# Two low parts per narrow-expert chunk move from VectorE to GpSimd, and TensorE takes them half a piece later

## The chip, the cores and the metric

The kernel runs on one core of a Trainium2 chip. Its engines each run their own queue of instructions: TensorE (PE, whose weight loads the profile calls PEld), VectorE (DVE), ScalarE (ACT), GpSimd (POOL) and SyncE (SP), which here issues the weight loads from memory. The metric is the device time of one execution in microseconds (us).

## What is computed

A decoder trunk of two layers over 256 tokens of width 1024: attention, a dense SwiGLU, an mLSTM mixer, and then the part that this change touches, a top-2-of-8 expert SwiGLU with a hidden width of 3584:

```python
def swiglu(h, wg, wu, wd):
    return (jax.nn.silu(h @ wg) * (h @ wu)) @ wd

def moe_swiglu(h, router, wg, wu, wd):
    ...
    for e in range(N_EXPERTS):
        y = y + combine[..., e:e + 1] * swiglu(h, wg[e], wu[e], wd[e]).astype(jnp.float32)
    return y.astype(h.dtype)
```

Everything is float32. The weights of all eight experts are read, 44 MB for each expert.

## The kernel before, in words

**Two parts for each number.** TensorE multiplies in the format fp32r, and the kernel keeps the accuracy by splitting each number into a high part (the number rounded to fp32r) and a low part (what the rounding left). For each weight, ScalarE makes the high part `whi` by a copy (line 204, in `split`), and VectorE makes the low part `wlo` by a subtraction of `whi` from the raw weight (line 208). Both inputs of that subtraction, `raw` and `whi`, lie in the on-chip memory SBUF.

**Experts, chunks, pieces, halves.** The eight experts come one after another, wide and narrow by turns (`WIDE`): a wide one has up to 128 tokens, a narrow one (1, 3, 5 and 7) up to 64. An expert has seven chunks of 512 hidden columns. A chunk loads six pieces of 1 MB: two of the gate matrix, two of the up matrix, two of the down matrix. Each piece is split and multiplied in two halves of 128x1024 numbers, so a chunk has twelve half pieces: gate 0 to 3, up 4 to 7, and then the four of the down product of the chunk before. In a narrow expert the stationary operand `xg` holds the high and the low part of 64 tokens side by side, so that a half piece takes four matmuls of 512 columns: two with `whi` (line 228) and then two with `wlo` (line 230), in `mm2s`. A wide expert takes six (lines 220, 221 and 223, in `mm3s`).

**The order.** `Stream.run` walks a list of half pieces, in an order that is kept on every engine. Before half piece n is multiplied, `fill` has issued the split of half piece n+3, so ScalarE and VectorE work up to three half pieces ahead. There are four buffers for `whi` and four for `wlo` (`NB_HI`, `NB_LO`), and ten for the raw pieces (`NB_RAW`): SyncE loads the next piece when both halves of an old one have been split. `Stream.soon(n, f)` puts a step off: it counts down at the end of each half piece, the present one too. Through it come, once for each narrow chunk, the turning of the two products onto the other axis (eight matmuls, line 1313), their product (VectorE, line 1320) and its low part (line 1325); in chunk 3 also the gathering of the next expert's tokens (line 1517), and after an expert's last chunk the scattering of its result (line 1445).

In `mm2s`, the matmuls of a narrow half piece:

```python
for o, l, r, start, _ in terms:
    nc.tensor.matmul(o, l, r[0], start=start, stop=False)
for o, l, r, _, stop in terms:
    nc.tensor.matmul(o, l, r[1], start=False, stop=stop)
```

GpSimd has no work in the experts' stretch but a small transfer and two products at the very end. Earlier, in the attention, it makes six low parts of weights (line 208 too) and one at line 599.

Of the kernel before, what the change touches and what calls it, by code (L numbers as in the profile page):

```python
# [23 lines left out]
KB = D // P  # L24
# [22 lines left out]
WIDE = (True, False, True, False, True, False, True, False)  # L47
# [22 lines left out]
def trunk(ctx: ExitStack, tc: tile.TileContext, out, rope_inv, x, positions, norm_mix, norm_ffn,  # L70
# [3 lines left out]
    nc = tc.nc  # L74
# [35 lines left out]
    def ps(tag, shape, dtype=F32):  # L110
        return psum.tile(shape, dtype, name=uniq("ps_" + tag), tag=tag, bufs=4)


    def load(src, shape, key=None):
        if key in early:
            return early.pop(key)
        n = int(np.prod(shape[1:]))
        t = weights.tile([P, 2048], F32, name=uniq("raw"), tag="raw", bufs=NB_RAW)
        v = t[:, :n]
        if len(shape) == 3:  # L120
            v = v.rearrange("p (k c) -> p k c", k=shape[1])
        nc.sync.dma_start(v, src)
        return v
# [18 lines left out]
    class Stream:  # L142
# [2 lines left out]
        def __init__(self):  # L145
            self.items, self.ready, self.later, self.at = [], [], [], 0

        def piece(self, src, shape, use, after=None, key=None):

            raw = []  # L150

            def get(j, sub):
                if not raw:
                    raw.append(load(None if key in early else src(), shape, key))
                v = raw[0]
                if isinstance(v, list):
                    return [w.rearrange("p a c -> p (a c)") for w in split(v[2 * j:2 * j + 2], sub)]
                return split(v[:, 2 * j:2 * j + 2] if shape[1] == 4 else v[:, j], sub)

            self.items.append((partial(get, 0), lambda w: use(0, w), None))  # L160
            self.items.append((partial(get, 1), lambda w: use(1, w), after))
# [25 lines left out]
    def split(v, sub=nc.vector):  # L187
        vs = v if isinstance(v, list) else [v]
        shape = [P, 2, 512] if isinstance(v, list) else list(v.shape)
        n = int(np.prod(shape[1:]))  # L190
        hi = weights.tile([P, 1024], F32R, name=uniq("whi"), tag="whi", bufs=NB_HI)[:, :n]
        lo = weights.tile([P, 1024], F32R, name=uniq("wlo"), tag="wlo", bufs=NB_LO)[:, :n]
        if len(shape) == 3:
            hi = hi.rearrange("p (k c) -> p k c", k=shape[1])
            lo = lo.rearrange("p (k c) -> p k c", k=shape[1])
        if chores and begun[0]:
            chores.pop(0)()
        with ExitStack() as order:
            if held:
                for ins in held.pop(0):  # L200
                    order.enter_context(tc.issue_after(ins))
            for i, part in enumerate(vs):
                h, l = (hi[:, i], lo[:, i]) if isinstance(v, list) else (hi, lo)
                nc.scalar.copy(h, part)  # L204
                if sub == PUT_OFF:
                    put_off.append(partial(nc.vector.tensor_sub, l, part, h.bitcast(F32)))
                elif sub:
                    sub.tensor_sub(l, part, h.bitcast(F32))  # L208
        return hi, lo
# [7 lines left out]
    def mm3s(terms):  # L217

        for o, l, r, start, _ in terms:
            nc.tensor.matmul(o, l[0], r[0], start=start, stop=False)  # L220
            nc.tensor.matmul(o, l[1], r[0], start=False, stop=False)  # L221
        for o, l, r, _, stop in terms:
            nc.tensor.matmul(o, l[0], r[1], start=False, stop=stop)  # L223

    def mm2s(terms):

        for o, l, r, start, _ in terms:
            nc.tensor.matmul(o, l, r[0], start=start, stop=False)  # L228
        for o, l, r, _, stop in terms:
            nc.tensor.matmul(o, l, r[1], start=False, stop=stop)  # L230


    ident = const([P, P], F32, "ident")
# [100 lines left out]
    def rsqrt_steps(ssq, scales, name):  # L334

        n = ssq.shape[1]
        v = tmp([P, n], F32, name + "_v")
        y = tmp([P, n], F32, name + "_y")
        t = tmp([P, n], F32, name + "_t")
        yi = y.bitcast(I32)  # L340
        steps = [partial(nc.vector.tensor_scalar, v[:, a:b], ssq[:, a:b], 1.0 / width, EPS, op0=OP.mult, op1=OP.add)
                 for a, b, width in scales]
        steps += [partial(nc.vector.tensor_scalar, yi, v.bitcast(I32), 1, None, op0=OP.logical_shift_right),
                  partial(nc.vector.tensor_scalar, yi, yi, -1.0, float(0x5F3759DF), op0=OP.mult, op1=OP.add)]
        each = [slice(i, i + 1) for i in range(n)]
        if n <= NT:
            steps.append(partial(nc.vector.tensor_scalar, v, v, -0.5, None, op0=OP.mult))
        for _ in range(3):
            if n <= NT:
                steps += [partial(nc.vector.scalar_tensor_tensor, t[:, c], y[:, c], v[:, c], y[:, c],  # L350
                                  op0=OP.mult, op1=OP.mult) for c in each]
                steps += [partial(nc.vector.scalar_tensor_tensor, y[:, c], t[:, c], 1.5, y[:, c],
                                  op0=OP.add, op1=OP.mult) for c in each]
            else:
                steps += [partial(nc.vector.scalar_tensor_tensor, t, y, -0.5, y, op0=OP.mult, op1=OP.mult),
                          partial(nc.vector.tensor_mul, t, t, v),
                          partial(nc.vector.scalar_tensor_tensor, y, t, 1.5, y, op0=OP.add, op1=OP.mult)]
        return y, steps

    def rsqrt_pool(ssq, width, name):  # L360

        v, y, t = (tmp(list(ssq.shape), F32, name + part) for part in ("_v", "_y", "_t"))
        yi = y.bitcast(I32)
        nc.vector.tensor_scalar(v, ssq, 1.0 / width, EPS, op0=OP.mult, op1=OP.add)
        nc.vector.tensor_scalar(yi, v.bitcast(I32), 1, None, op0=OP.logical_shift_right)
        nc.vector.tensor_scalar(yi, yi, -1.0, float(0x5F3759DF), op0=OP.mult, op1=OP.add)
        nc.gpsimd.tensor_scalar(v, v, -0.5, None, op0=OP.mult)
        for _ in range(3):
            nc.gpsimd.tensor_mul(t, y, v)
            nc.gpsimd.tensor_mul(t, t, y)  # L370
            nc.gpsimd.tensor_scalar(t, t, 1.5, None, op0=OP.add)
            nc.gpsimd.tensor_mul(y, y, t)
        return y
# [56 lines left out]
    def at(pair, *idx):  # L430
        return pair[0][idx], pair[1][idx]
# [158 lines left out]
    r, more = rsqrt_steps(ssq, [(0, NT, Q_LORA), (NT, 2 * NT, KV_LORA)], "lat")  # L590
# [25 lines left out]
    def q_rotary(wq4, b):  # L616
        p = ps("a", [P, 4, ROPE])
        for k in range(2):
            mm3(p, tok(cT, k, b), at(wq4[k], slice(None), slice(None), slice(NOPE, QK)), k == 0, k == 1)
        return p  # L620
# [7 lines left out]
    for a in range(2):  # L628
        for b in range(NT):
            nc.tensor.matmul(rows_p[:, a, b * P:(b + 1) * P], r[:, 2 * a + b:2 * a + b + 1].to_broadcast([P, P]), ident,  # L630
                             start=True, stop=True)
# [65 lines left out]
    for half in range(2):  # L697
# [6 lines left out]
        for b in range(NT):  # L704
            p = q_rotary(wq4, b) if half else qr_first[b]
# [3 lines left out]
        for h in range(hs, hs + 4, 2):  # L709
            p = ps("a", [P, 2, S])  # L710
# [6 lines left out]
        for h in range(hs, hs + 4, 2):  # L717
            p = ps("a", [P, 2, S])
# [3 lines left out]
        for b in range(NT):  # L722
            p = ps("a", [P, 4, VD])
# [52 lines left out]
    piece = []  # L776
# [60 lines left out]
    r = x_ffn.rsqrt("ffn0")  # L837
# [79 lines left out]
    for k in range(KB):  # L917
        for n in range(2):
            nc.tensor.matmul(rows_p, wg[:, k].rearrange("p a c -> p (a c)"), aT[n][:, k],
                             start=k + n == 0, stop=k == KB - 1 and n == 1)  # L920
# [35 lines left out]
    for blocks, src in ((slice(0, 2), Mr), (slice(2, 3), Mr[:, P:])):  # L956
        n = src.shape[1] // P
        src = src.rearrange("p (a c) -> p a c", a=n)
# [43 lines left out]
    for h in range(HEADS):  # L1002
        e = ps("b", [P, 3, P])
# [3 lines left out]
                         start=False, stop=True)  # L1007
# [30 lines left out]
    r = rsqrt_pool(hsq, VD, "head")  # L1038
# [211 lines left out]
    def expert_chunk(e, c):  # L1250

        for w, after in ((moe_w_gate, gated), (moe_w_up, upped)):
            p = []
            for i in range(2):
                moe.piece(lambda w=w, i=i: w[expert_at(e), c, i], [P, 4, 512], partial(inner, e, i, p),
                          partial(after, e, c, p) if i else None)

    def inner(e, i, p, j, w):
        if i + j == 0:
            p.append(ps("a", [P, 512]))  # L1260
        xg = tokens[e][0]
        k = 4 * i + 2 * j
        if not WIDE[e]:
            mm2s([(p[0], xg[:, k + kk], at(w, slice(None), kk), k + kk == 0, k + kk == KB - 1) for kk in range(2)])
            return
        mm3s([(p[0], (xg[:, 0, k + kk], xg[:, 1, k + kk]), at(w, slice(None), kk), k + kk == 0, k + kk == KB - 1)
              for kk in range(2)])
# [179 lines left out]
    moe = Stream()  # L1447
# [103 lines left out]
    xg = bigt([P, KB, P], F32, "xg")  # L1551
    with tc.If(rv > 0):
        for e in range(NE):
# [5 lines left out]
            for c in range(NCH):  # L1559
                gu = []  # L1560
                for w in (moe_w_gate[e], moe_w_up[e]):
                    p = ps("a", [P, 512])
# [14 lines left out]
                for i in range(2):  # L1577
                    raw = load(moe_w_down[e, 2 * c + i], [P, 2, D])
                    for h in range(2):
                        for kk in range(2):  # L1580
                            j = 2 * i + kk
                            nc.tensor.matmul(acc[h], hT[:, j], raw[:, kk, h * 512:(h + 1) * 512],
                                             start=c == 0 and j == 0, stop=c == NCH - 1 and j == 3)
            for h in range(2):
                ye = tmp([P, 512], F32, "ye_hi")
                nc.scalar.copy(ye, acc[h])
                for b in range(NT):
                    p = ps("a", [P, 512])
# [61 lines left out]
```

## Time and profile before

| what | value |
|---|---|
| time, median of 3 runs | 1414.47 us (1413.94 to 1414.93) |
| the profiled execution's own time | 1414.09 us |
| its span in the profile | 1412.4 us |
| experts' stretch, first to last narrow chunk | about 575 to 1395 us of the span |
| busy: PE, DVE, ACT, POOL | 97%, 88%, 71%, 4% of the span |
| TensorE's granted clock, mean over the span | 0.995 |
| read from memory | 436.67 MB, 310 GB/s over the span |

The span is the time from the first to the last instruction of the profiled execution; 1.7 us of its own time lie outside it. A busy share is the time in which an engine had an instruction in work. The matmuls overlap each other in the record, so that TensorE counts as busy when it is not at its peak. Line numbers are those of the kernel before; those of the change lie up to eight lines later.

### The profile page before, as it was taken

The page shows a single profiled execution, that of the slowest core. Times are in us where ns is not written, and L with a number is a line of the kernel's source. Part 1 is how long each engine was busy: PE and PEld are TensorE (multiplying, and loading weights), DVE is VectorE, ACT ScalarE, POOL GpSimd, SP SyncE. Part 2 cuts the span into 40 slices and gives each one's busy share as a digit, 9 for nine tenths or more (in the row PEclk, how much of TensorE's full clock was granted, in tenths as well). Part 3 has the DMA queues.
Part 4 walks back from the last instruction along what each step waited for, and adds up shares of the span by engine and source line. Part 5 has one row for each costly group of instructions (what it writes and reads, how often), then busy time and mean ns, then how long its engine had stood idle before and what let it go on. Part 6 is the DMA issues. An engine that isn't in the chain of part 4 may idle for free.

```text
span 1412.4 us, 18954 instructions
## 1 busy us (share of the span) xinstructions
PE 1363.4 (97%) x6457; PEld 1086.2 (77%) x6457; DVE 1249.6 (88%) x1604; ACT 999.1 (71%) x1272; POOL 51.4 (4%) x99
## 2 busy tenths in 40 slices
PE   7999999999999899999999999999999999999995
PEld 5788888888887688877778877778887777888673
DVE  6859998956978888999998899999889999899996
ACT  5545444445864777888877788977788897778995
POOL 4300000000020100000000000000000000000000
PEclk9999999999999999999999999999999999999998
DMA  9456666555457777999999999999999999999991
GB/s 361 160 209 208 212 211 218 194 180 197 175 197 309 275 291 266 353 368 390 421 380 338 352 368 412 399 420 365 335 366 370 400 416 399 334 371 380 381 416 36
DMA packets 63614, 439.06 MB, mean 311 GB/s; under 512 B 7489, under 2 KB 7654, under 8 KB 11798
## 3 DMA queue, kind: packets, MB, share of 16 engines
q1 hardware_dynamic: 61478, 428.15, 79.2%
q0 software_dynamic: 1872, 9.61, 1.9%
q8 instruction: 52, 0.85, 0.2%
q14 instruction: 52, 0.43, 0.1%
q10 hardware_dynamic: 160, 0.02, 0.0%
HBM read 436.67 MB, written 1.08 MB: 310 GB/s over the span
## 4 chain that ended last, share of the span: by engine, by line
PE 84%; DVE 9%; issue 2%; ACT 2%; POOL 1%; DMA 0%; DVEq 0%; ACTq 0%; POOLq 0%
PE ps_a L220 11%; PE ps_a L221 11%; PE ps_a L223 11%; PE ps_a L230 6%; PE ps_a L228 5%; PE ps_b L230 4%; DVE wlo L208 4%; PE ps_b L220 4%; PE ps_b L228 4%; PE ps_b L221 4%; PE ps_b L223 3%; PE ps_a L1313 3%; PE ps_b L213 3%; PE ps_b L215 3%; PE ps_b L214 3%
## 5 line engine op out<-in xcount | busy, mean ns | idle before, releaser
L208 DVE TENSOR_TENSOR wlo<-raw,whi 128x1024 fp32r<-128x1024 f32 (+1 forms) x783 | 919.8, 1224 | 96.5 <-ACT whi L204 91.1
L204 ACT CAST whi<-raw 128x1024 fp32r<-128x1024 f32 (+1 forms) x792 | 804.1, 1049 | 256.2 <-PE ps_a L221 112.2
L220 PE MATMUL ps_a<-whi,xg 128*128 128x512 f32 x448 | 177.0, 395 | 1.1 <-ACT whi L204 1.1
L221 PE MATMUL ps_a<-whi,xg 128*128 128x512 f32 x448 | 176.3, 393 | 0.0
L230 PE MATMUL ps_a<-wlo,xg 128*128 128x512 f32 x448 | 147.8, 411 | 8.3 <-DVE wlo L208 8.2
L223 PE MATMUL ps_a<-wlo,xg 128*128 128x512 f32 x448 | 140.2, 394 | 1.9 <-DVE wlo L208 1.9
L228 PE MATMUL ps_a<-whi,xg 128*128 128x512 f32 x448 | 140.2, 394 | 0.0
L230 PEld LDWEIGHTS ps_a<-wlo,xg 128*128 128x128 f32 x448 | 77.4, 188 | 50.8 <-DVE wlo L208 38.3
L223 PEld LDWEIGHTS ps_a<-wlo,xg 128*128 128x128 f32 x448 | 83.8, 188 | 22.7 <-DVE wlo L208 3.2
L220 PEld LDWEIGHTS ps_a<-whi,xg 128*128 128x128 f32 x448 | 84.1, 188 | 21.0 <-ACT whi L204 1.5
L221 PEld LDWEIGHTS ps_a<-whi,xg 128*128 128x128 f32 x448 | 84.1, 188 | 19.7 <-DVE xg L1517 0.5
L228 PEld LDWEIGHTS ps_a<-whi,xg 128*128 128x128 f32 x448 | 84.0, 188 | 19.2
L220 PE MATMUL ps_b<-whi,hT_hi 128*128 128x512 f32 x224 | 91.2, 407 | 0.0
L220 PE MATMUL ps_a<-whi,xT_hi 128*128 128x512 f32 x224 | 88.5, 395 | 0.1
L221 PE MATMUL ps_b<-whi,hT_lo 128*128 128x512 f32 x224 | 88.4, 394 | 0.0
L221 PE MATMUL ps_a<-whi,xT_lo 128*128 128x512 f32 x224 | 88.3, 394 | 0.0
L768 DVE CUSTOM_DVE_ANT_0 junk<-raw,wr 128x1024 bf16<-128x1024 f32 x64 | 78.1, 1221 | 2.0 <-DMA raw<-mlstm_w_out_dram 1.4
L230 PE MATMUL ps_b<-wlo,hT_hi 128*128 128x512 f32 x224 | 75.4, 416 | 0.5 <-DVE wlo L208 0.5
L228 PE MATMUL ps_b<-whi,hT_hi 128*128 128x512 f32 x224 | 73.2, 406 | 1.0 <-ACT whi L204 1.0
L223 PE MATMUL ps_b<-wlo,hT_hi 128*128 128x512 f32 x224 | 70.3, 395 | 0.0
L223 PE MATMUL ps_a<-wlo,xT_hi 128*128 128x512 f32 x224 | 69.9, 392 | 0.0
L213 PE MATMUL ps_b<-whi,hT_hi 128*128 128x512 f32 x152 | 60.9, 401 | 0.0
(443 smaller groups left out, 1882.2 us busy)
## 6 DMA issues: line engine op xcount, KB each, us to landing
raw<-moe_w_gate_dram SPq DMA_DIRECT2D x112, 1024.0 KB, 6.3
raw<-moe_w_up_dram SPq DMA_DIRECT2D x112, 1024.0 KB, 6.8
raw<-moe_w_down_dram SPq DMA_DIRECT2D x105, 1024.0 KB, 7.3
raw<-ffn_w_gate_dram SPq DMA_DIRECT2D x14, 1024.0 KB, 4.9
raw<-ffn_w_up_dram SPq DMA_DIRECT2D x14, 1024.0 KB, 5.1
raw<-ffn_w_down_dram SPq DMA_DIRECT2D x14, 1024.0 KB, 4.8
raw<-mlstm_w_in_dram SPq DMA_DIRECT2D x12, 1024.0 KB, 4.8
raw<-mla_w_out_dram SPq DMA_DIRECT2D x4, 1024.0 KB, 7.7
```

The costliest lines, as they stand in the source:

```text
L204: nc.scalar.copy(h, part)
L208: sub.tensor_sub(l, part, h.bitcast(F32))
L213: nc.tensor.matmul(o, l[0], r[0], start=start, stop=False)
L214: nc.tensor.matmul(o, l[0], r[1], start=False, stop=False)
L215: nc.tensor.matmul(o, l[1], r[0], start=False, stop=stop)
L220: nc.tensor.matmul(o, l[0], r[0], start=start, stop=False)
L221: nc.tensor.matmul(o, l[1], r[0], start=False, stop=False)
L223: nc.tensor.matmul(o, l[0], r[1], start=False, stop=stop)
L228: nc.tensor.matmul(o, l, r[0], start=start, stop=False)
L230: nc.tensor.matmul(o, l, r[1], start=False, stop=stop)
L768: nc.vector.tensor_tensor_reduce(junk, a, b, 1.0, 0.0, OP.mult, OP.add, acc)
L1313: nc.tensor.matmul(t[:, n, j], src[:, j * P:(j + 1) * P], twice, start=n + j == 0, stop=n + j == 4)
```

## The change

In a narrow expert, the low part of the second half of the first gate piece (half piece 1) and of the first up piece (half piece 5) is made on GpSimd in place of VectorE: 2 of the 12 half pieces of a chunk, 56 in all. The same subtraction of the same shape goes to another queue. For half piece 1 and 5 of a narrow chunk, the two matmuls with the low part are put off by `soon(2)`, which is to the end of the next half piece.

```diff
-        def piece(self, src, shape, use, after=None, key=None):
+        def piece(self, src, shape, use, after=None, key=None, on_pool=None):
...
             def get(j, sub):
+                if j == on_pool:
+                    sub = nc.gpsimd
...
-    def mm2s(terms):
+    def mm2s(terms, later=None):
 
         for o, l, r, start, _ in terms:
             nc.tensor.matmul(o, l, r[0], start=start, stop=False)
-        for o, l, r, _, stop in terms:
-            nc.tensor.matmul(o, l, r[1], start=False, stop=stop)
+
+        def low_parts():
+            for o, l, r, _, stop in terms:
+                nc.tensor.matmul(o, l, r[1], start=False, stop=stop)
+
+        later(low_parts) if later else low_parts()
...
-                          partial(after, e, c, p) if i else None)
+                          partial(after, e, c, p) if i else None, on_pool=None if WIDE[e] or i else 1)
...
-            mm2s([(p[0], xg[:, k + kk], at(w, slice(None), kk), k + kk == 0, k + kk == KB - 1) for kk in range(2)])
+
+            mm2s([(p[0], xg[:, k + kk], at(w, slice(None), kk), k + kk == 0, k + kk == KB - 1) for kk in range(2)],
+                 partial(moe.soon, 2) if (i, j) == (0, 1) else None)
```

On VectorE, in the gate and the first up half pieces of one chunk of expert 1, before (`raw_5559` and `raw_5588` are the two gate pieces, `raw_5609` and `raw_5629` the up pieces; a `wlo` is a low part):

```order
L208 TENSOR_TENSOR wlo_5562<-raw_5559,whi_5561 128x1024
L208 TENSOR_TENSOR wlo_5581<-raw_5559,whi_5580 128x1024
L208 TENSOR_TENSOR wlo_5591<-raw_5588,whi_5590 128x1024
L1320 TENSOR_TENSOR hT_lo_5579<-ps_a_5569,hT_lo_5579 128x256
L208 TENSOR_TENSOR wlo_5601<-raw_5588,whi_5600 128x1024
L208 TENSOR_TENSOR wlo_5612<-raw_5609,whi_5611 128x1024
L1325 TENSOR_TENSOR hT_hi_5578<-hT_lo_5579,hT_hi_5578 128x4x64
L208 TENSOR_TENSOR wlo_5622<-raw_5609,whi_5621 128x1024
L208 TENSOR_TENSOR wlo_5632<-raw_5629,whi_5631 128x1024
```

The same place on VectorE with the change:

```order
L210 TENSOR_TENSOR wlo_5562<-raw_5559,whi_5561 128x1024
L210 TENSOR_TENSOR wlo_5591<-raw_5588,whi_5590 128x1024
L1328 TENSOR_TENSOR hT_lo_5579<-ps_a_5569,hT_lo_5579 128x256
L210 TENSOR_TENSOR wlo_5601<-raw_5588,whi_5600 128x1024
L210 TENSOR_TENSOR wlo_5612<-raw_5609,whi_5611 128x1024
L1333 TENSOR_TENSOR hT_hi_5578<-hT_lo_5579,hT_hi_5578 128x4x64
L210 TENSOR_TENSOR wlo_5632<-raw_5629,whi_5631 128x1024
```

`wlo_5581` and the second half of `raw_5609` have gone from VectorE's queue. They now stand on GpSimd's, one behind the other with nothing between, for all narrow chunks of an expert.

On TensorE, the four gate half pieces of the same chunk, before:

```order
L228 MATMUL ps_a_5604<-whi_5561,xg_4725 128x512 x2
L230 MATMUL ps_a_5604<-wlo_5562,xg_4725 128x512 x2
L228 MATMUL ps_a_5604<-whi_5580,xg_4725 128x512 x2
L230 MATMUL ps_a_5604<-wlo_5581,xg_4725 128x512 x2
L228 MATMUL ps_a_5604<-whi_5590,xg_4725 128x512 x2
L230 MATMUL ps_a_5604<-wlo_5591,xg_4725 128x512 x2
L228 MATMUL ps_a_5604<-whi_5600,xg_4725 128x512 x2
L230 MATMUL ps_a_5604<-wlo_5601,xg_4725 128x512 x2
```

And with the change:

```order
L230 MATMUL ps_a_5604<-whi_5561,xg_4725 128x512 x2
L234 MATMUL ps_a_5604<-wlo_5562,xg_4725 128x512 x2
L230 MATMUL ps_a_5604<-whi_5580,xg_4725 128x512 x2
L230 MATMUL ps_a_5604<-whi_5590,xg_4725 128x512 x2
L234 MATMUL ps_a_5604<-wlo_5591,xg_4725 128x512 x2
L234 MATMUL ps_a_5604<-wlo_5581,xg_4725 128x512 x2
L230 MATMUL ps_a_5604<-whi_5600,xg_4725 128x512 x2
L234 MATMUL ps_a_5604<-wlo_5601,xg_4725 128x512 x2
```

The two matmuls with `wlo_5581` have moved behind all four of half piece 2. Their number is the same.

## Rows read from the trace of the kernel before

**Rows 1.** The page's parts 1 and 5: engines, costliest groups.

```profile
PE 1363.4 (97%) x6457; PEld 1086.2 (77%) x6457; DVE 1249.6 (88%) x1604; ACT 999.1 (71%) x1272; POOL 51.4 (4%) x99
...
L208 DVE TENSOR_TENSOR wlo<-raw,whi 128x1024 fp32r<-128x1024 f32 (+1 forms) x783 | 919.8, 1224 | 96.5 <-ACT whi L204 91.1
```

**Rows 2.** Busy time by chunk: a wide one, expert 1's, one of expert 7.

```profile
core 0: us, PE busy (x) PEld busy (x) DVE busy (x) ACT busy (x) POOL busy (x), PEclk, DMA share, GB/s
558.20:575.39 17.19, 17.19 (x77) 13.93 (x76) 15.25 (x15) 13.39 (x14) 0.00 (x0) 1.00 0.96 368
575.39:590.68 15.29, 15.29 (x69) 12.41 (x68) 13.73 (x16) 13.24 (x16) 0.00 (x0) 1.00 0.85 303
590.68:608.05 17.37, 17.05 (x81) 13.58 (x80) 16.79 (x19) 14.32 (x19) 0.00 (x0) 1.00 0.98 388
608.05:623.20 15.15, 14.21 (x67) 10.48 (x65) 15.15 (x16) 13.23 (x16) 0.00 (x0) 1.00 0.85 321
623.20:637.49 14.29, 14.01 (x66) 10.33 (x65) 14.29 (x15) 13.14 (x18) 0.00 (x0) 1.00 1.01 423
637.49:656.08 18.59, 17.71 (x104) 14.90 (x104) 16.64 (x20) 14.52 (x22) 0.00 (x0) 1.00 0.98 391
...
684.37:700.33 15.96, 15.68 (x72) 11.76 (x72) 15.96 (x17) 13.54 (x18) 0.00 (x0) 1.00 1.01 420
...
1336.90:1351.19 14.29, 14.04 (x65) 10.36 (x65) 14.29 (x15) 13.12 (x18) 0.00 (x0) 1.00 1.01 420
```

**Rows 3.** Timeline of VectorE in one chunk of expert 7: start, length, line.

```profile
1337.02 11.45 DVE L208 TENSOR_TENSOR wlo<-raw,whi 128x1024 fp32r<-128x1024 f32 x10
1348.37 0.43 DVE L1320 TENSOR_TENSOR hT_lo<-ps_a,hT_lo 128x256 f32<-128x256 f32 x1
1348.70 2.37 DVE L208 TENSOR_TENSOR wlo<-raw,whi 128x1024 fp32r<-128x1024 f32 x2
```

**Rows 4.** Timeline of TensorE in the same chunk, first waiting, then not.

```profile
1339.44 0.30 PEld L230 LDWEIGHTS ps_a<-wlo,xg 128*128 128x128 f32 x2 [0.37 <-DVE wlo L208]
...
1343.41 1.00 PE L1313 MATMUL ps_a<-twice,act 128*128 128x64 f32 x8
...
1345.11 0.71 PE L228 MATMUL ps_b<-whi,hT_hi 128*128 128x512 f32 x2
...
1348.00 0.63 PE L228 MATMUL ps_a<-whi,xg 128*128 128x512 f32 x2
1348.46 0.63 PE L230 MATMUL ps_a<-wlo,xg 128*128 128x512 f32 x2
```

**Rows 5.** Timeline of GpSimd's low parts in the attention, some merged.

```profile
18.60 2.19 POOL L208 TENSOR_TENSOR wlo<-raw,whi 128x896 fp32r<-128x896 f32 x1 [11.70 <-ACT whi L204]
...
24.32 2.35 POOL L599 TENSOR_TENSOR wlo<-raw,whi 128x1024 fp32r<-128x1024 f32 x1
...
39.02 4.19 POOL L208 TENSOR_TENSOR wlo<-raw,whi 128x768 fp32r<-128x768 f32 x2 [4.30 <-ACT whi L204]
```

**Rows 6.** Timeline of VectorE beside those of group 5.

```profile
17.72 1.09 DVE L208 TENSOR_TENSOR wlo<-raw,whi 128x896 fp32r<-128x896 f32 x1
18.73 2.08 DVE L516 SCALAR_TENSOR_TENSOR mix_y<-mix_t,mix_y 128x1 f32<-128x1 f32 x1
...
24.39 2.30 DVE L516 SCALAR_TENSOR_TENSOR mix_y<-mix_t,mix_y 128x1 f32<-128x1 f32 x1
...
39.17 1.81 DVE L478 TENSOR_TENSOR qr<-rope_u,rope_v 128x128 f32<-128x128 f32 x1
...
41.10 0.68 DVE L714 TENSOR_TENSOR qkT<-ps_a,rows 128x512 f32<-128x512 f32 x1
41.70 1.66 DVE L478 TENSOR_TENSOR qr<-rope_u,rope_v 128x128 f32<-128x128 f32 x1
```

**Rows 7.** All of line 208 on GpSimd and of line 478: ns min/median/max.

```profile
L208 POOL TENSOR_TENSOR wlo<-raw,whi x6: 1812/1851/2416, 18.6 to 40.8; 128x768 fp32r<-128x768 f32 x4, 128x896 fp32r<-128x896 f32 x1, 128x1024 fp32r<-128x1024 f32 x1
...
L478 DVE TENSOR_TENSOR qr<-rope_u,rope_v x8: 282/284/1814, 37.8 to 52.0; 128x128 f32<-128x128 f32 x8
```

## The prediction

> **What bounds the kernel now.** I read the page first. TensorE is busy for 97% of the span and VectorE for 88% [rows 1]; a busy TensorE is no proof, since its matmuls overlap in the record. So I cut the experts' stretch into chunks, each from one gate product's reading to the next, and read each engine's busy time in it [rows 2]. A wide chunk takes 17.19 us with TensorE at 17.19 and VectorE at 15.25: TensorE is the limit. A steady narrow chunk takes 14.29 us, and there VectorE is busy for all 14.29, ScalarE for 13.14, while the memory queues move 423 GB/s at a share of 1.01.
>
> The timeline of a narrow chunk says the same. VectorE makes ten low parts in a row from 1337.02 to 1348.37 [rows 3], 1.135 us from one to the next, with no idle time. Twelve of them are 13.6 us, and the product and its low part (0.33 each, as from 1348.37 to 1348.70) bring it to 14.29. TensorE could go faster: where it waits for nothing, it begins a pair of matmuls every 0.46 to 0.47 us (1348.00 to 1348.46), 0.233 for one, and the eight turning matmuls take 1.70 us (1343.41 to 1345.11); 48 x 0.233 + 1.70 = 12.9 us a chunk. In the slow part it waits 0.37 us for a low part in each half piece [rows 4]. VectorE is thus the bound of the narrow chunks, and a change in its load there goes straight into the time.
>
> **The change, part by part.** *Removed from VectorE:* two subtractions a chunk, 2 x 1.135 = 2.27 us [rows 3], 56 in all. *Added on GpSimd:* the same 56. The trace has one such shape that began alone, 2.35 us at line 599 [rows 5], and one right behind another, 2.416 us, the longest of line 208 on GpSimd [rows 7]. I take 2.38.
>
> *What the two do to each other* decides. Look at what VectorE did while GpSimd subtracted in the attention. At 18.60 GpSimd began 2.19 us of work [rows 5]; at 18.73 VectorE began an operation on one number per partition, with two inputs in SBUF, and it took 2.08 us, to 20.81, just past GpSimd's end at 20.79 [rows 6]. At 24.39 another such one took 2.30 us, to 26.69, and GpSimd's end was 26.67. Line 478, which reads two SBUF tensors, has a median of 284 ns and a longest of 1814 [rows 7]: the long ones are those at 39.17 and 41.70 [rows 6], beside the two GpSimd operations from 39.02 on [rows 5]. Between them line 714, which reads one input from PSUM and one from SBUF, ran in 0.68 us with GpSimd at work throughout. So a VectorE operation with two SBUF inputs stands still while GpSimd subtracts and ends 0.02 to 0.15 us after it, whatever its size; one with a single SBUF input doesn't notice. The low parts of the weights read `raw` and `whi`, both in SBUF. They are of the kind that stops, and they are nearly all that VectorE does in a narrow chunk.
>
> Who goes first? At 18.60 GpSimd's operation came up while VectorE still had a subtraction in work (17.72 to 18.81), and VectorE's next, at 18.73, was the one that stood still [rows 5, 6]. So the waiting GpSimd operation got its turn before VectorE's next; I take it that the 56 slip in likewise.
>
> Then the two engines are one queue as far as low parts go. Each moved operation gives VectorE 1.135 us and takes 2.38: 1.245 us net. For a steady chunk that is 14.29 + 2.49 = 16.78 us. VectorE stays the bound in it, with ScalarE at 13.1 and TensorE at 12.9.
>
> A rule of the Trainium skill speaks against this change too (SBUF — State Buffer, Who interferes with whom): GpSimd and a VectorE instruction with two SBUF inputs contend for one read interface, and the one that begins first holds it for its whole length. The rows agree for GpSimd going first; that a VectorE subtraction holds up GpSimd alike is hardly shown by them. The same page (A bandwidth-pool intuition that's wrong) puts the release at about 115 ns after the holder's end; the rows have 20 ns for the tiny operations. By the page each hand-over would add some 0.1 us, 6 us over 56; I go by the rows.
>
> *Moved on TensorE:* 112 matmuls behind the next half piece's four. Their number stays; the four come 0.93 us sooner and the two as much later, which TensorE's slack of 14.29 less 12.9 covers. If that cover were gone, 56 x 0.47 = 26 us would be the most. *Buffers:* the low part of half piece 1 is held until after half piece 2, so a later low part waits for it. VectorE has three subtractions between (of half pieces 2, 3 and 4), 3.4 us, in which TensorE has caught up: nothing as long as GpSimd gets its turn early. *The loads:* a raw piece is let go up to 2.4 us later; the ten of them hold a chunk and two thirds, 24 us of work, which covers it. SyncE's loads are asked for at a slower rate, and the queues get air. GpSimd's own queue holds nothing else there but one small transfer that is needed at the end.
>
> *Where it is hidden.* Not every narrow stretch is full [rows 2]. From 575.39 to 590.68 TensorE is the limit and VectorE idles for 1.56 us: the first moved operation of an expert costs nothing there. From 590.68 to 608.05 it idles for 0.58, and in the chunk that gathers the next expert's tokens (637.49 to 656.08) for 1.95; that idle time lies in short waits, and I take half of it, 0.98. The other stretches are full, the one that ends at 700.33 too. So for one expert 13 x 1.245 - 0.58 - 0.98 = 14.6 us. Experts 3 and 5 are built alike. Expert 7 has no next one to gather for and runs its chunks at 14.29 (the last row of group 2): 13 x 1.245 - 0.58 = 15.6. Sum: 3 x 14.6 + 15.6 = 59.4 us.
>
> The profiled execution took 1414.09 us, 1.7 more than its span and within 0.4 of the median, 1414.47. 1414.1 + 59.4 = 1473.5 us.
>
> **Bounds.** Low: GpSimd's operation may begin while VectorE's last one drains (0.2 us of overlap at 18.60, of which its own length took back some 0.1), 2.25 us and 1.1 net; all of the 1.95 usable; and the product (0.33, one SBUF input) always under a GpSimd operation, 27 x 0.33 = 9 us: 3 x 11.8 + 13.7 - 9 = 40 us. High: 2.5 us a piece with hand-overs, 1.37 net, no idle time of use: 56 x 1.37 = 77 us. That is 1454 to 1491.
>
> **The rivals.**
> *A. The two don't stop each other in this stretch (faster).* Then VectorE falls to 12.0 us a chunk and ScalarE sets 13.1, 1.2 us less for some seven chunks of four experts: 33 us. The memory queues stand against that: 12 half pieces are 6.29 MB, 440 GB/s at 14.29 us, already more than the 423 that they move at a share of 1.01, so the gain draws on the ten raw buffers. I put it at 20 to 33, 1381 to 1394 us. The break-even is a GpSimd operation that stops VectorE for no more than 1.135 of its 2.38 us. Against it: every two-input operation of group 6 stood still to the end. Chance 4%.
> *B. GpSimd gets no turn while VectorE has work (slower still).* VectorE would run on to the low part that needs the buffer of half piece 1, and stop; GpSimd works for 2.38 us with VectorE idle, and then TensorE must do 0.47 + 0.93 us before the buffers come free, in which the second moved operation can block once more. About 1.1 us a chunk more: 56 x 1.245 + 28 x 1.1 = 100 us, 1514. Against it is the turn taken at 18.60. Chance 10%. The skill's rule above, that the first to begin holds the lock, gives GpSimd its turn only if VectorE's next instruction hasn't taken it by then.
> *C. Cheap collisions.* GpSimd's operations drift to where VectorE waits or reads PSUM anyway, and half of the cost is hidden: +10 to +40, 1424 to 1454. VectorE has no idle time in the full chunks to drift to. Chance 6%.
> *D. No change that can be measured:* gain and loss would have to cancel. 2%. That the change does nothing is out: the order of VectorE's queue has 56 rows fewer.
>
> **How the numbers follow.** The forecast, one queue for both, has 78%: 1473.5 us, its own range 1454 to 1491. For 8 in 10 I take 1446 to 1504: down into C, up towards B. Two thirds of A, C and D and half of B stay out, less than 2 in 10. A difference of 0.2%, 2.8 us, is about what a measurement of this kernel can tell from none. Faster by more: 0.04 (A). Within it: 0.02 (D). Slower: 0.94 (the forecast, B, C).
>
> **What would show it.** In the profile after: GpSimd with some 185 us busy (51.4 + 56 x 2.38), more if its spans contain waits; line 208 on VectorE with 727 instructions and, among them, up to 56 of 3.4 to 3.6 us in place of 1.22, each ending about 1.1 us after a GpSimd operation; VectorE busy for all of a steady narrow chunk of 16.6 to 16.9 us; the memory rate down to about 375 GB/s there; wide chunks at 17.2 as before. B would show as VectorE idle before low parts, waiting for TensorE, and chunks near 17.9; A as narrow chunks of 13.1 to 14 us with subtractions of 1.22 us beside GpSimd's. I am wrong if VectorE's subtraction is not held as the small operations were.

## The result, and the profile after

The changed kernel takes 1481.78 us (median of 4 runs, 1479.76 to 1490.45) against 1414.70 us for the one before, 4.8% more: the ratio is 1.0481, with a 95% interval of 1.0463 to 1.0499. The prediction was 1473.5 us in a range of 1446 to 1504. The profiled execution took 1482.05 us, 68 more than that of before.

The page of the changed kernel, part 1, to be held against [rows 1]: GpSimd's busy time has gone from 51 to 219 us, and VectorE, with 56 instructions fewer, is busy for 24 us more.

```profile
PE 1373.6 (93%) x6457; PEld 1101.1 (74%) x6457; DVE 1273.7 (86%) x1548; ACT 1004.1 (68%) x1272; POOL 218.7 (15%) x155
```

Busy time by chunk of the changed kernel, cut at the same instruction as [rows 2]. The rows are the first stretch of expert 3, two full chunks of it, the one that gathers, and two of expert 7:

```profile
core 0: us, PE busy (x) PEld busy (x) DVE busy (x) ACT busy (x) POOL busy (x), PEclk, DMA share, GB/s
827.16:842.47 15.31, 15.31 (x69) 12.40 (x68) 12.46 (x12) 13.07 (x14) 3.47 (x2) 1.00 0.97 341
...
861.80:879.01 17.21, 13.90 (x66) 10.47 (x64) 16.46 (x15) 13.33 (x17) 5.82 (x3) 1.00 0.91 333
879.01:895.45 16.44, 13.84 (x65) 10.40 (x64) 15.69 (x14) 13.31 (x17) 6.36 (x3) 1.00 0.98 377
895.45:917.55 22.10, 19.44 (x103) 16.27 (x102) 17.03 (x18) 14.62 (x21) 5.44 (x3) 0.92 0.85 294
...
1393.86:1411.18 17.32, 15.32 (x65) 11.68 (x64) 15.24 (x14) 13.30 (x18) 5.68 (x3) 0.90 0.97 365
1411.18:1427.61 16.43, 13.90 (x65) 10.39 (x64) 15.67 (x14) 13.31 (x17) 6.35 (x3) 1.00 0.98 381
```

A steady narrow chunk has gone from 14.29 to 16.44 us, the full one before it from 15.2 to 17.21; the first stretch, where TensorE is the limit, is 15.3 us as before. The chunk that gathers takes 22.10 us in place of 18.59, and there, and in one of expert 7's two chunks, TensorE's granted clock is not 1.00.

Timelines of VectorE and GpSimd in a chunk of expert 7 with the clock at 1.00, which answer to [rows 3]:

```profile
1376.21 1.22 DVE L210 TENSOR_TENSOR wlo<-raw,whi 128x1024 fp32r<-128x1024 f32 x1
1377.35 2.61 DVE L1333 TENSOR_TENSOR hT_hi<-hT_lo,hT_hi 128x256 fp32r<-128x256 f32 x1
1379.88 8.03 DVE L210 TENSOR_TENSOR wlo<-raw,whi 128x1024 fp32r<-128x1024 f32 x7
1388.65 2.61 DVE L210 TENSOR_TENSOR wlo<-raw,whi 128x1024 fp32r<-128x1024 f32 x1 [0.74 <-ACT whi L206]
1391.19 0.41 DVE L1328 TENSOR_TENSOR hT_lo<-ps_a,hT_lo 128x256 f32<-128x256 f32 x1
```

```profile
1376.63 3.05 POOL L210 TENSOR_TENSOR wlo<-raw,whi 128x1024 fp32r<-128x1024 f32 x1 [2.88 <-ACT whi L206]
1386.87 3.32 POOL L210 TENSOR_TENSOR wlo<-raw,whi 128x1024 fp32r<-128x1024 f32 x1 [7.19 <-ACT whi L206]
```

Both directions of the stop can be read here. GpSimd's first subtraction came up at 1376.63, while VectorE had one in work since 1376.21; it took 3.05 us, to 1379.68. VectorE's next, the small one at line 1333, stood from 1377.35 to 1379.96. First that line in the kernel before, where its median is 427 ns, then now (ns min/median/max):

```profile
L1325 DVE TENSOR_TENSOR hT_hi<-hT_lo,hT_hi x28: 418/427/446, 607.4 to 1390.1; 128x256 fp32r<-128x256 f32 x28
L1333 DVE TENSOR_TENSOR hT_hi<-hT_lo,hT_hi x28: 407/2610/2642, 613.3 to 1457.9; 128x256 fp32r<-128x256 f32 x28
```

The second moved operation came up at 1386.87, waited for VectorE until about 1387.9 and ran to 1390.19. VectorE idled for 0.74 us of that, since its next `whi` was not there yet, and stood in a subtraction for the rest. All low parts of weights, VectorE's and GpSimd's (ns min/median/max; GpSimd's six of the attention are among them):

```profile
L210 DVE TENSOR_TENSOR wlo<-raw,whi x727: 1085/1218/3416, 12.7 to 1459.9; 128x1024 fp32r<-128x1024 f32 x181, 128x896 fp32r<-128x896 f32 x1
L210 POOL TENSOR_TENSOR wlo<-raw,whi x62: 1807/3040/3489, 18.6 to 1443.9; 128x1024 fp32r<-128x1024 f32 x57, 128x768 fp32r<-128x768 f32 x4, 128x896 fp32r<-128x896 f32 x1
```

### The profile page after: what moved, and what is told of

It reads as the page before. It is cut to its first block, busy times and chain, and to the rows that moved or that the text cites. A ratio compares the mean times of both kernels' runs of the same rounds, so it can differ in the third digit from the quotient of the medians.

```text
span 1480.2 us, 19070 instructions
## 1 busy us (share of the span) xinstructions
PE 1373.6 (93%) x6457; PEld 1101.1 (74%) x6457; DVE 1273.7 (86%) x1548; ACT 1004.1 (68%) x1272; POOL 218.7 (15%) x155
## 3 DMA queue, kind: packets, MB, share of 16 engines
HBM read 436.67 MB, written 1.08 MB: 296 GB/s over the span
## 4 chain that ended last, share of the span: by engine, by line
PE 77%; DVE 10%; issue 6%; ACT 5%; POOL 1%; DMA 0%; DVEq 0%; ACTq 0%; POOLq 0%
PE ps_a L222 10%; PE ps_a L223 10%; PE ps_a L225 10%; PE ps_a L234 5%; DVE wlo L210 5%; PE ps_b L234 4%; ACT whi L206 4%; PE ps_b L230 4%; PE ps_b L222 3%; PE ps_b L223 3%; PE ps_b L225 3%; PE ps_a L1321 3%; PE ps_a L230 3%; PE ps_b L217 3%; PE ps_b L215 3%
## 5 line engine op out<-in xcount | busy, mean ns | idle before, releaser
L210 DVE TENSOR_TENSOR wlo<-raw,whi 128x1024 fp32r<-128x1024 f32 (+1 forms) x727 | 890.3, 1263 | 133.2 <-ACT whi L206 127.8
L210 POOL TENSOR_TENSOR wlo<-raw,whi 128x1024 fp32r<-128x1024 f32 (+2 forms) x62 | 179.0, 2890 | 830.3 <-ACT whi L206 807.7
L234 PE MATMUL ps_a<-wlo,xg 128*128 128x512 f32 x448 | 143.9, 424 | 59.5 <-DVE wlo L210 59.5
L222 PE MATMUL ps_a<-whi,xg 128*128 128x512 f32 x448 | 177.1, 395 | 1.1 <-ACT whi L206 1.1
L223 PE MATMUL ps_a<-whi,xg 128*128 128x512 f32 x448 | 176.2, 393 | 0.0
L234 PEld LDWEIGHTS ps_a<-wlo,xg 128*128 128x128 f32 x448 | 80.7, 194 | 102.6 <-DVE wlo L210 89.2
L225 PE MATMUL ps_a<-wlo,xg 128*128 128x512 f32 x448 | 140.3, 394 | 1.9 <-DVE wlo L210 1.9
L230 PE MATMUL ps_a<-whi,xg 128*128 128x512 f32 x448 | 134.6, 400 | 0.0
L225 PEld LDWEIGHTS ps_a<-wlo,xg 128*128 128x128 f32 x448 | 83.8, 188 | 22.7 <-DVE wlo L210 3.2
L222 PE MATMUL ps_b<-whi,hT_hi 128*128 128x512 f32 x224 | 91.3, 407 | 0.0
L230 PE MATMUL ps_b<-whi,hT_hi 128*128 128x512 f32 x224 | 74.8, 414 | 1.0 <-ACT whi L206 1.0
```

## The experiments

**Is it the two engines' meeting, or the low parts that come late?** Two runs took one half of the change each. The first leaves the low parts on VectorE and only puts them off on TensorE:

```diff
             def get(j, sub):
-                if j == on_pool:
-                    sub = nc.gpsimd
```

> The change without GpSimd: VectorE makes all twelve low parts, TensorE takes those of half pieces 1 and 5 half a piece later. Theory 1 (GpSimd's subtraction stops VectorE's): the order on TensorE costs nothing, the time is that of the kernel before, 1414 us, within 3, and a steady narrow chunk is 14.3 us. Theory 2 (the loss comes from the low part that is held longer, from its buffer and from TensorE's waits): a loss of 10 to 26 us shows here already.

It took 1417.49 us, a ratio of 1.0014 (1.0004 to 1.0023), with steady chunks of 14.29 us. The order on TensorE by itself costs about 2 us, some 3 at most. The second moves the low parts and leaves TensorE's order as it was:

```diff
-            mm2s([...], partial(moe.soon, 2) if (i, j) == (0, 1) else None)
+            mm2s([...])
```

> The change without the putting off: GpSimd makes the two low parts, TensorE takes each in its old place. Theory 1: the two engines' sum is the same, a steady narrow chunk 16.4 to 16.8 us, the time 1478 to 1495 us. Theory 2: without the putting off TensorE stands before every one of GpSimd's low parts, so the time goes well above 1495 us.

1473.72 us (1.0393 to 1.0430 of before). A steady chunk of it:

```profile
1385.80:1402.21 16.41, 14.89 (x65) 10.10 (x64) 15.66 (x14) 13.31 (x18) 6.65 (x3) 1.00 0.99 384
```

That is the steady chunk of the changed kernel, so most of the loss is in the moving. But it is 8 us faster than the whole change, less than either theory had allowed for: putting off helps nothing and hurts somewhere. More on that below.

**VectorE reads one SBUF input.** The changed kernel, in which VectorE's ten subtractions of a narrow chunk take a constant tile in PSUM in place of `whi`, so that they no longer wait for ScalarE either; GpSimd, its buffers and TensorE's order are those of the change:

```diff
+                elif sub == nc.vector and narrow:
+                    ...
+                    sub.tensor_sub(l2, p2, flat[0][:, None, :].to_broadcast([P, 2, 512]))
```

> The changed kernel, in which VectorE's own subtractions in the narrow experts take their second input from a constant tile in PSUM in place of whi; GpSimd's read SBUF as before. The low parts that come out are not the true ones. Theory 1: with one SBUF input VectorE isn't stopped, its subtractions last 1.2 to 1.3 us beside GpSimd's, and a steady narrow chunk takes 13.1 to 14 us, 1385 to 1415 us in all. Theory 2: nothing changes in GpSimd's time, in the buffers and on TensorE, so 16.4 us a chunk and about 1480 us stay.

1383.28 us, 0.9774 of the kernel before (0.9757 to 0.9792): the loss of 67 us has turned into a gain. That is a little under the 1385 to 1415 us that were expected. A steady chunk, timelines of VectorE and of GpSimd in a narrow chunk of this run, then all such subtractions of VectorE (ns min/median/max):

```profile
1326.16:1339.12 12.96, 12.96 (x65) 10.79 (x64) 12.07 (x13) 12.96 (x18) 4.84 (x3) 1.00 1.01 421
```

```profile
1325.33 8.00 DVE L213 TENSOR_TENSOR wlo<-raw,ps_b 128x1024 fp32r<-128x1024 f32 x7
1334.22 1.22 DVE L213 TENSOR_TENSOR wlo<-raw,ps_b 128x1024 fp32r<-128x1024 f32 x1 [0.89 <-PE ps_b L239]
```

```profile
1325.39 2.42 POOL L215 TENSOR_TENSOR wlo<-raw,whi 128x1024 fp32r<-128x1024 f32 x1 [1.95 <-ACT whi L208]
1333.99 2.42 POOL L215 TENSOR_TENSOR wlo<-raw,whi 128x1024 fp32r<-128x1024 f32 x1 [6.18 <-ACT whi L208]
```

```profile
L213 DVE TENSOR_TENSOR wlo<-raw,ps_b x278: 1205/1211/1223, 584.9 to 1361.7; 128x1024 fp32r<-128x1024 f32 x139
```

GpSimd's two take 2.42 us each and VectorE works on beside them, no subtraction longer than 1.223 us. The chunk is 12.9 to 13.0 us, the pace that was worked out for TensorE. The control is the same edit on the kernel before, with no GpSimd in it:

> The kernel before, in which VectorE's subtractions of the narrow experts take their second input from a constant tile in PSUM, as in the run with GpSimd before this; the control for it. If that subtraction costs VectorE what the true one does, a steady narrow chunk is 14.2 to 14.4 us and the whole 1412 to 1418 us, and what the other run gained is the gain of moved work that stops nobody, not of cheaper subtractions.

One run, 1407.61 us, steady chunks of 14.25 us, subtractions of 1.21 us. These cost VectorE what the true ones do; the 8 us below the kernel before (1415.57 us beside this run) lie in the other chunks, 13.32 in place of 14.00 us in the one behind the gathering for one. That these don't wait for ScalarE may be why; it was not tested. Against this control the moving gained 24 us. The cause of the loss is thus shown: it needs VectorE's second SBUF input, and GpSimd's time, the buffers and the order alone don't make it.

**More work on GpSimd, whose result nobody waits for.** On the kernel before, after half piece 1 and 5 of a narrow chunk have been split:

```diff
+                if j == more:
+                    nc.gpsimd.tensor_sub(v[:, 2:4], v[:, 2:4], w[0].bitcast(F32))
```

> The kernel before, in which GpSimd does two subtractions of 128x1024 more in a narrow chunk, in place on a raw half piece that has been split already, with nothing waiting for their result. No work is taken from VectorE. Theory 1: each stops VectorE for 2.1 to 2.4 us, 56 of them 105 to 135 us less what lies in idle time: 1510 to 1540 us, a steady chunk of 18.4 to 19 us. Theory 2: nobody waits for these, so the time stays near 1415 us.

1555.77 us, 1.0986 (1.0965 to 1.1007): 140 us for 56 operations, 2.5 each, above the 1510 to 1540 us that were expected. Not all of it is the price of the reading. The granted clock was 0.955 over the span, and the added operation holds the `whi` buffer that it reads: ScalarE, which fills it next, waited for GpSimd 26 times, with 5.4 us as the longest:

```profile
ACT whi L207 <- POOL raw L160: 67.6, 26, 5.4
```

A chunk with the clock at 1.00, in which VectorE is busy throughout, shows the price by itself, 3.8 us more than 14.29 for two operations, 1.9 each:

```profile
1463.52:1481.61 18.09, 14.32 (x65) 10.25 (x64) 18.09 (x15) 13.22 (x18) 6.55 (x2) 1.00 0.89 328
```

The same with two fillings with zeros in its place:

```diff
+                    for _ in range(2):
+                        nc.gpsimd.memset(v[:, 2:4], 0.0)
```

> The same places, but GpSimd fills the half piece with zeros twice, about 2.1 us by the 0.54 us of its filling of 128x512 in the trace of before: as long on GpSimd, and nothing read. Theory 1 in its narrow form (GpSimd's reading of SBUF stops VectorE's two-input operations): 1413 to 1420 us, VectorE's subtractions 1.22 us. If any work on GpSimd stops VectorE: 1500 us or more.

1419.60 us, 1.0025 (1.0015 to 1.0036), steady chunks of 14.29. Of each of the two runs, first the one that reads and then the one that writes, GpSimd's group at the added work (count, busy us, mean ns) and all of VectorE's low parts (ns min/median/max):

```profile
L160 POOL TENSOR_TENSOR raw<-raw,whi 128x1024 f32<-128x1024 f32 x56 | 170.0, 3036 | 883.6 <-DVE wlo L211 577.4 <-issue 166.6 <-DMA raw<-moe_w_up_dram 131.5
```

```profile
L211 DVE TENSOR_TENSOR wlo<-raw,whi x783: 1083/1217/3404, 12.4 to 1534.7; 128x1024 fp32r<-128x1024 f32 x195, 128x896 fp32r<-128x896 f32 x1
```

```profile
L161 POOL MEMSET raw<- 128x1024 f32 x112 | 107.1, 957 | 812.3 <-DVE wlo L212 677.4 <-DMA raw<-moe_w_up_dram 131.8
```

```profile
L212 DVE TENSOR_TENSOR wlo<-raw,whi x783: 1084/1217/1228, 12.6 to 1395.8; 128x1024 fp32r<-128x1024 f32 x195, 128x896 fp32r<-128x896 f32 x1
```

107 us of writing on GpSimd leave VectorE's longest low part at 1.228 us; 170 us of reading bring it to 3.404. It is GpSimd's reading that stops VectorE. The 4 us that the writing cost lie in the chunks that gather (19.3 to 21.0 us in place of 18.6, the longest with the granted clock at 0.92); why was not looked into.

**What a free GpSimd would be worth.** The two low parts are not made, on the kernel before; TensorE multiplies by the low part of the half piece before in their place, so that its work is the same:

```diff
+                if j == left_out:
+                    return split(v[:, 2 * j:2 * j + 2], "none")[0], first[0][1]
```

> The kernel before, in which the low parts of half pieces 1 and 5 of a narrow chunk are not made at all; TensorE multiplies by the low part of the half piece before in their place, so that its work is the same. This is the change with a GpSimd that costs nothing. Theory 1, with VectorE as the bound of the narrow chunks: 14.29 us falls to 13.1 to 13.8, where ScalarE or the loads take over, 1385 to 1402 us. If VectorE is not what bounds them: 1414 us.

1393.09 us, 0.9846 (0.9829 to 0.9864), a steady chunk of 13.45 us in which VectorE is busy for 12.29. VectorE was the bound, and the loads (422 GB/s at a share of 1.01, as before) didn't take over: in the run with the PSUM tile they let chunks of 13.0 us through.

**Half the dose.** The gate piece alone:

```diff
-                          ..., on_pool=None if WIDE[e] or i else 1)
+                          ..., on_pool=1 if not WIDE[e] and i == 0 and w is moe_w_gate else None)
```

> The change for the gate piece alone: one low part of a narrow chunk on GpSimd, put off on TensorE. Theory 1, a cost for each moved operation: half of the loss, 1440 to 1450 us, a steady chunk of 15.2 to 15.5 us. Theory 3 (most of the loss is what comes with TensorE's long waits, its granted clock): well under half, since the waits for the up pieces that delay the gathering are gone: 1430 to 1440 us.

1438.41 us, 1.0163 (1.0145 to 1.0181), in the range that was expected if part of the loss comes with TensorE's waits. Its steady chunk:

```profile
1357.74:1373.11 15.37, 14.57 (x65) 10.18 (x64) 14.62 (x15) 13.21 (x17) 3.57 (x1) 1.00 1.01 421
```

In the steady chunk the loss is half to the hundredth, 1.08 us against 2.15 for two. In the whole it is a third, 23 of 67 us. So some 20 us of the full change are not the price of its operations one by one.

**Where those are.** In the changed kernel TensorE does the high parts of half pieces 5 and 6 without a stop and then waits for VectorE's low part of half piece 6, which stood behind line 1333; the put-off low part of half piece 5 comes right behind it. TensorE around such a wait, twice, 16 us apart:

```profile
1381.15 1.20 PE L234 MATMUL ps_a<-wlo,xg 128*128 128x512 f32 x4 [2.00 <-DVE wlo L210]
1382.18 0.63 PE L230 MATMUL ps_a<-whi,xg 128*128 128x512 f32 x2
...
1397.59 2.06 PE L234 MATMUL ps_a<-wlo,xg 128*128 128x512 f32 x4 [2.00 <-DVE wlo L210]
1399.45 1.05 PE L230 MATMUL ps_a<-whi,xg 128*128 128x512 f32 x2
```

And the stretches of the second wait, TensorE alone (busy, granted clock, share and rate of the loads):

```profile
1395.00:1398.00 3.00, 1.00 (x4) 0.94 0.94 311
1398.00:1401.00 3.00, 3.00 (x8) 0.50 0.96 380
```

After the same stop of 2.00 us the matmuls go on as ever in the first, and at half the rate in the second; the granted clock from 1398 to 1401 is 0.50, the lower of its two levels, 1.2 GHz. It costs that chunk 0.9 us (17.32 against 16.43). Without the putting off, TensorE waits in that place for 1.04 us, for GpSimd, and 0.21 us more for VectorE, and expert 7 has no chunk below 1.00. In the chunk that gathers, the chain is longer: the stopped line 1333 holds up the comparison that makes the gathering's operand, and TensorE waits for it, 0.60 us in expert 3 of the kernel before and 2.66 us now; there it then works at the lower level:

```profile
873.95 2.05 PE L1509 MATMUL ps_a<-oh,x_gain 128*128 128x128 f32 x16 [0.60 <-DVE oh L1215]
...
899.38 3.62 PE L1517 MATMUL ps_a<-oh,x_gain 128*128 128x128 f32 x16 [2.66 <-DVE oh L1221]
```

What the clock took can be added up, since each kind of stretch also occurs at 1.00. Of the changed kernel, the chunk that gathers in expert 1, the second stretch of experts 3 and 7, and the last full chunk of expert 7:

```profile
648.22:668.35 20.13, 17.67 (x103) 14.58 (x101) 16.61 (x17) 14.62 (x21) 5.02 (x3) 1.00 0.88 310
842.47:861.80 19.33, 17.19 (x81) 13.58 (x80) 17.35 (x17) 14.68 (x18) 6.99 (x3) 1.00 0.97 369
1339.11:1360.24 21.13, 18.77 (x81) 14.80 (x80) 17.41 (x17) 14.61 (x18) 5.27 (x3) 0.92 0.92 335
1427.61:1444.71 17.10, 15.09 (x65) 11.66 (x64) 15.04 (x14) 13.31 (x18) 5.70 (x3) 0.90 0.54 200
```

Seven chunks are below 1.00. Each is longer than its like at 1.00 in the same execution: those that gather in experts 3 and 5 by 2.0 us each, three of expert 7 by 1.8, 0.9 and 0.7, two of expert 1 by 0.5 and 0.2. That is 8 us, what the whole change lost against the moving alone. Over the span the granted clock was 0.988 to 0.993 in the four runs of the moving alone and 0.972 to 0.984 in those of the whole change.

Two runs tried to take this away. One fills the wait with six matmuls of no use, between the high and the low part of half pieces 2 and 6:

```diff
+        if busy:
+            keep_warm(6)
```

> The changed kernel with six matmuls of no use in the place where TensorE waits for the put-off low parts, between the high and the low part of half pieces 2 and 6. Theory 1: a steady chunk stays at 16.4 us. Theory 3 (part of the loss, some 8 us, is TensorE's granted clock that falls after a wait of 2 us): the granted clock is 0.99 or more in the chunks where it fell to 0.90, none of them over 16.5 us, and the time is 1470 to 1476 us. If the clock has nothing to do with those waits: 1480 us, or more with the added matmuls on the path.

Expert 7's chunks from the second on, of this run:

```profile
1360.81:1376.38 15.57, 15.57 (x77) 11.83 (x76) 14.35 (x12) 13.33 (x17) 5.11 (x3) 1.00 0.84 317
1376.38:1392.36 15.98, 15.98 (x77) 11.64 (x76) 15.22 (x13) 13.32 (x16) 5.89 (x3) 1.00 0.98 375
1392.36:1408.82 16.46, 16.00 (x77) 11.65 (x76) 15.72 (x13) 13.43 (x17) 6.38 (x3) 1.00 0.98 382
1408.82:1425.26 16.44, 15.98 (x77) 11.65 (x76) 15.69 (x13) 13.43 (x17) 6.35 (x3) 1.00 0.97 382
1425.26:1441.71 16.45, 15.99 (x77) 11.65 (x76) 15.69 (x13) 13.42 (x17) 6.37 (x3) 1.00 0.60 233
```

All at 1.00 and none over 16.5: for these five, 80.9 us in place of 84.5. The whole came only to 1477.57 us (1.0415 to 1.0446 of before), just above the 1470 to 1476 us that were expected. The chunks that gather did not gain: 23.9 us in expert 1, at 0.93, and 22.5 us in experts 3 and 5, although the clock was 1.00 there; that the added matmuls lie on the path in them was not tested. The other run left the up piece of the gathering chunk to VectorE:

```diff
+    def gathers(e, c, w):
+
+        return c == 3 and e + 1 < NE and w is moe_w_up
...
-                          ..., on_pool=None if WIDE[e] or i else 1)
+                          ..., on_pool=None if WIDE[e] or i or gathers(e, c, w) else 1)
```

> The changed kernel, in which the up piece of the chunk that gathers the next expert's tokens (chunk 3 of experts 1, 3 and 5) is left to VectorE. Theory 3: the gathering waited for VectorE's comparison behind a stopped subtraction; that chunk falls from 20.1 to 22.1 us to 19 to 20 us, and the whole to 1472 to 1478 us. Theory 1 alone, three moved operations fewer: 1478 us, each worth 1.1 to 1.2 us.

Those chunks fell to 18.7 to 19.1 us, at or below the 19 to 20 that were expected, and the whole to 1476.01 us (1471.67 to 1479.36). But the granted clock was lower elsewhere, 0.974 over the span of the profiled run, with narrow chunks of 17.1 to 17.6. Why the clock is lost in some chunks and not in their like stays open.

**A version that relieves VectorE without GpSimd.** On the kernel before, half piece 1 isn't split; TensorE multiplies it whole:

```diff
+        if w[1] is None:
+            for kk in range(2):
+                nc.tensor.matmul(p[0], xg[:, k + kk].bitcast(F32), w[0][:, kk], start=False, stop=False)
+            return
```

> The kernel before, in which half piece 1 of a narrow chunk isn't split: TensorE multiplies the raw float32 weights by the float32 tokens, at a quarter of the rate, which is 8 x 0.104 us for 8 x 64 columns in the rows at line 1313, so 0.83 us for 512 columns; two of them 1.66 us in place of 0.93. VectorE loses one subtraction a chunk (13.15 us), TensorE comes to 13.65 us, ScalarE to 12.1. If VectorE's load goes straight into the time, a steady narrow chunk takes 13.6 to 13.8 us and the whole 1396 to 1405 us; if the loads bound it as soon as VectorE is eased, 1408 to 1414 us.

1411.98 us, 0.9975 of before (0.9963 to 0.9988): a little faster than both kernels, but not the 1396 to 1405 us that were expected if VectorE's load went straight into the time. It lies where a bound by the loads was expected, but the chunk shows another limit. Its steady chunk:

```profile
1363.25:1377.30 14.05, 14.05 (x65) 10.67 (x64) 13.34 (x14) 12.29 (x16) 0.00 (x0) 1.00 0.92 373
```

VectorE has come down to 13.34 us and TensorE is the new limit, 0.4 us above the 13.65 that were worked out.

## Why the prediction was right

*VectorE bounds the narrow chunks.* Right: two low parts fewer bring 14.29 to 13.45 us, 22 us in all. It is not the bound by much: of the 2.27 us taken from it, 0.84 came out.

*The two engines are one queue for operations with two SBUF inputs.* Right, and it carries the result. One input from PSUM, with GpSimd's work as in the change, turned +67 into -32 us; GpSimd's reading costs a full chunk 1.9 us for each operation where nobody waits for its result, and its writing nothing. The Trainium skill's rule (SBUF — State Buffer, Who interferes with whom) goes as far as that: it names the second SBUF input, and a GpSimd instruction that only writes as harmless. Both show here, 3.404 against 1.228 us as the longest low part. The other direction, which the rows of before hardly showed, is there too: GpSimd's operation takes 2.42 us undisturbed and 3.05 to 3.32, in the chunk shown, when it must wait for VectorE first.

*GpSimd gets its turn.* Right for this kernel: in the chunk shown, VectorE's next operation stood still until the waiting GpSimd was done, no GpSimd operation took over 3.489 us, which is its 2.42 and less than one subtraction, and VectorE had no wait for TensorE before its low parts in the narrow chunks. It is no rule, as the last section shows. Rival B, with 17.9 us a chunk, did not come, nor did A or C.

*The price.* 1.245 us net for each operation was somewhat too much in the full chunks: 2.15 us for two, 1.08 each, just below the lower bound of 1.1. From 1377.35 to 1379.88 VectorE spent 2.53 us on an operation that fills 0.33 or so, 2.2 us for GpSimd's in place of 2.38. An estimate of why: with 2.42 us of its own, GpSimd's operation, which ended at 1379.68, began at about 1377.26, and VectorE's subtraction before it is on record until 1377.43; so the two overlap where one follows the other. The Trainium skill (SBUF — State Buffer, A bandwidth-pool intuition that's wrong (but worth ruling out)) has a release about 115 ns after VectorE's end, measured on a DMA whose descriptors GpSimd writes. Added to each hand-over here, it would have gone the wrong way.

*Where it is hidden.* Right for the first operation of an expert (15.31 us, no change) and about right for the next stretch (2.0 us where 1.9 was said). For the chunk that gathers, 2.49 less 0.98, 1.5 us more, was said. In expert 1, with the clock at 1.00, it took 1.5 us more; that this is the number is in part luck, since at the true price of 2.15 only 0.6 us was hidden. The idle time there is a chain of waits, and the stopped operation stood in it. In experts 3 and 5 it took 3.5 us more, with the granted clock at 0.92.

*The putting off costs nothing.* Wrong in size: it is nearly free alone (2 us) and in a steady chunk (16.44 against 16.42), but with VectorE's low part late as well it collects TensorE's waits into one of 2 us, after which the granted clock at times falls to the lower level. The whole change is 8 us slower than the moving alone, and the clock was no term of the sum.

*The signs.* VectorE has 727 instructions at the line of the low parts, and the memory queues move 377 GB/s in the steady chunk, as was said. GpSimd is busy for 219 us and not 185, with its waits in its spans, which had been allowed for. Not as said: the steady chunk is 16.44 us and not 16.6 to 16.9, VectorE is busy for 15.69 of them and not for all, and only four low parts took 3.4 us. In the experts' stretch 50 operations of VectorE took over 1.4 us: line 1333 24 times, with 2.6 us, those four low parts, and 22 more of 1.7 to 2.6 us, which came up when GpSimd had already begun.

Added up for the profiled run: 14.3, 15.5 and 15.5 us in experts 1, 3 and 5 (14.6 each predicted), 18.8 in expert 7 to the end (15.6), and 3.7 us before the experts begin, where both kernels run the same instructions and the granted clock of the first 80 us was 0.91 in place of 0.96. That is 68 us against 59.4. Without the 8 us that the clock took in the narrow chunks and the 3.7 us ahead of them it would be 56, so the price, a little too high, and the clock, not foreseen, pulled in opposite directions. That the sum came as near as this is in part luck.

## What to carry to other kernels

Before work goes from VectorE to GpSimd, look at what VectorE does at that time: if its operations read two inputs from SBUF and GpSimd's read SBUF, the two don't run beside each other, and a busy VectorE loses GpSimd's longer time. One short operation of VectorE that took as long as GpSimd's, anywhere in the trace, is enough to see it. In these runs work moved to GpSimd paid where VectorE took one input from PSUM (24 us less than the control). GpSimd's writing, 107 us of it, cost 4 us, and the first moved operation of an expert, where TensorE is the limit and VectorE has slack, cost nothing.

## What was not expected of the hardware

After stops of TensorE of equal length (2.00 us) the granted clock stayed at 1.00 once and fell to 0.50 for some 3 us the next time. The four runs of the changed kernel show it over the span: 0.972 at 1490.45 us, 0.981 to 0.984 at 1479.76 to 1482.05, against 0.995 for the profiled run of before.

GpSimd's turn is not sure. In the run with more reading, four of its 56 added operations, one in each narrow expert, took 5.5 us. One of them, and VectorE beside it:

```profile
887.98 5.54 POOL L160 TENSOR_TENSOR raw<-raw,whi 128x1024 f32<-128x1024 f32 x1 [9.06 <-DVE wlo L211]
```

```profile
886.70 4.61 DVE L211 TENSOR_TENSOR wlo<-raw,whi 128x1024 fp32r<-128x1024 f32 x4
```

VectorE's four subtractions run through without a stop to 891.31, and GpSimd's operation ends 2.2 us after them. So VectorE began two more while GpSimd stood, which is what rival B supposed. Why it got past here and not in the changed kernel stays open.
